# Sixteen gate projections spread anew over the attention units of a two-layer decoder trunk

## The chip, the cores and the metric

One core of one Trainium2 chip. The metric is the device time of one launch in microseconds (us), the median of the runs. Engines: PE (matrix products; PEld is its weight load), DVE (vector), ACT (scalar functions), POOL (GpSimd), SP (issues transfers). PE's clock has two levels, 1.2 and 2.4 GHz; the profile gives the granted share.

## The reference

Two layers, 512 tokens, width 1024, everything in float32:

```python
h = rms_norm(x, g_attn)
proj = h @ w_in                       # dq dk dv sq sk sv gates: 6 x 512 + 2 x 1024 columns
o_diff = diff_attention(...)          # 4 heads: softmax(q1 k1) - lam * softmax(q2 k2), rotary on q and k
o_sb = stick_breaking_attention(...)  # 8 heads: running product of sigmoids along the keys
g_diff, g_sb = split(sigmoid(gates + b_gate))
merged = g_diff * (o_diff @ w_o_diff) + g_sb * (o_sb @ w_o_sb)
x = x + merged @ w_out
gate, up = split(rms_norm(x, g_ffn) @ w_ffn_in)
x = x + (silu(gate) * up) @ w_ffn_out
```

A last RMSNorm ends the trunk.

## The kernel before, in words

All activations lie transposed, with 128 channels on the partitions and the 512 tokens along a row. A product keeps float32 accuracy by splitting both operands into a high and a low part: each 128x512 step is three matmuls (lines 204, 205, 206: high times high, low weight times high, high weight times low). One *group* is 128 output columns over 8 blocks of the input, 24 matmuls of 512 columns into one PSUM bank.

The weights come as one stream of 512 KB pieces in the order of `layer_order`. For each, SP loads `wr`, ACT makes the high part `wh` (line 111), and DVE the low part `wl` (line 113). Of the input projection's pieces every fourth in the stream (`n % 4 == 0`) has its low part made by POOL instead. Two buffers hold `wr`, four each hold `wh` and `wl`, and two pieces are fetched ahead.

In a layer the input projection has 40 groups: three (k, q, v) for each of eight attention *units*, and 16 gate groups. Units s0 to s3 are stick-breaking, with two heads each; d0 to d3 are differential, with one head each. The groups of s0 open the layer. Then come eight *slots*, n = 0 to 7: slot n runs the score maps of unit n, the groups of unit n+1, and, `LAG` = 2 half slots later, the products with v of the unit before. `FILL[n]` says up to how many groups slot n holds; what is left after the three of unit n+1 is filled with gate groups. Gate groups that no slot takes stand in `TAIL`: two go beside the last two half slots, the rest behind all units. The 8 groups `ws`/`wd` of the output projections follow (12 matmuls each), with the sigmoids of the gates, then `w_out` and the FFN.

In `gate_group` (`pg` in the profile) the 24 matmuls fill a bank of tag `mm`, of which there are three, shared with the k, q and v groups. DVE then multiplies the bank by the norm's factor into a tile `gt` (line 321), and that frees the bank. Banks of tag `at` (five) hold scores (`ss`, `sd`), transposes (`ts`, `td`, `vts`, `vtd`), products with v (`avs`, `avd`) and the mean squares (`omd`). In the tile names a final s or d stands for the kind of unit.

The order written in the code is not the order of issue: a planner orders each engine's queue at build time from its own costs, and each engine then runs its queue in order. A matmul whose input is late therefore holds up all matmuls behind it.

Before the change, slots 0 to 3 hold three groups each (no gates), slots 4 to 6 one gate each, slot 7 four, and `TAIL` nine, of which seven stand behind all units. Only the first four gates get a tile of their own (`blk`); later ones reuse tiles of tag `stk`, `klz` and `wk` as units release them.

Of the kernel before, what the change touches and what calls it, by code (L numbers as in the profile page):

```python
# [15 lines left out]
P = 128  # L16
DEPTH = 2
S = 512
# [13 lines left out]
C_NA, C_NF, C_NL, C_BG, C_SL, C_LP = 0, 16, 32, 40, 72, 74  # L32


BUFS = dict(mx=4, sm=4, blk=12, tmp=5, stk=6, v=3, wk=4, wT=3)
BANK_BUFS = dict(mm=3, at=5)
W_BUFS, W_AHEAD = 4, 2
GATES_IN_BLK = 4
FILL = (3, 3, 3, 3, 4, 4, 4, 4)
LAG = 2  # L40


# [5 lines left out]
def trunk(ctx: ExitStack, tc, xT, par, tab, scn, msk, w_in, w_o, w_out, w_fi, w_fo, out):  # L48
    nc = tc.nc
# [6 lines left out]
    def bank(tag, name):  # L56
        return psm.tile([P, 512], F32, name=name, tag=tag, bufs=BANK_BUFS[tag])
# [4 lines left out]
    def unit_groups(u):  # L62
        kind, i = u
        return [("in", c + i) for c in ((4, 0, 8) if kind == "d" else (16, 12, 20))]
# [7 lines left out]
    for n in range(8):  # L72
        g = unit_groups(UNITS[n + 1]) if n < 7 else []
        while len(g) < FILL[n] and gi < len(GATES):
            g.append(GATES[gi])
# [118 lines left out]
    def mm(dst, key, rhs, first=True, last=True):  # L194

        hi, lo = w_get(*key)
        mm_tiles(dst, hi, lo, rhs, first, last)
# [70 lines left out]
    for l in range(DEPTH):  # L268
        h = nrm.h
        with ExitStack() as ac:  # L270
# [10 lines left out]
            def T(tag, name, shape=(P, S), dt=F32):  # L281
                return ap_.tile(list(shape), dt, name=f"{name}_{l}", tag=tag, bufs=BUFS.get(tag, 1))

            def blk(name, dt=F32):
                return T("blk", name, dt=dt)
# [13 lines left out]
                    nc.gpsimd.memset(f32(klz[b][c])[64 - 64 * c:128 - 64 * c], 0.0)  # L299

            gates = {}
            pair = [None]
            TAIL = list(TAIL0)

            def gate_group(key):
                b = bank("mm", f"pg{key[1]}_{l}")
                mm(b, (l,) + key, h)
                j = key[1] - 24
                n = len(gates)
                if n < GATES_IN_BLK:  # L310
                    t = blk(f"gt{j}")
                elif n < GATES_IN_BLK + BUFS["stk"]:
                    t = T("stk", f"gt{j}")
                elif n < GATES_IN_BLK + BUFS["stk"] + 2:
                    t = T(f"klz0{n - GATES_IN_BLK - BUFS['stk']}", f"gt{j}")
                else:
                    q = (n - GATES_IN_BLK - BUFS["stk"]) % 2
                    if q == 0:
                        pair[0] = T("wk", f"gt{j}", (P, 1280))
                    t = pair[0][:, q * S:q * S + S]  # L320
                nc.vector.tensor_tensor(out=t, in0=b, in1=r, op=ALU.mult)
                gates[j] = t

# [220 lines left out]
            def fill(key):  # L544
                n = sum(u.done == 3 for u in units)
                if n < 8 and key in unit_groups(UNITS[n]):
                    units[n].group(key)
                else:
                    gate_group(key)
# [34 lines left out]
            for m in range(8):  # L584
# [11 lines left out]
                nc.vector.tensor_tensor(out=gd, in0=gd, in1=gs, op=ALU.add)  # L596
                if m < 3 or m - 3 < BUFS["wk"] - 2:
                    t = T("wT" if m < 3 else "wk", f"mt{m}", (P, 1280), F32R)
# [122 lines left out]
```

## Time and profile before

| | |
|---|---|
| runs | 1520.3, 1525.24, 1525.61 us; median 1525.24 |
| profiled execution | 1526.8 us, of which the span from first to last instruction is 1525.0 |
| granted PE clock, mean over the span | 0.988 |
| PE busy | 1488.5 us |
| DVE, ACT, POOL busy | 853.7, 614.4, 347.4 us |
| attention stage of layer 0, of layer 1 | about 25 to 314 us, 770 to 1065 us |

How to read it: PE is busy nearly all the time, so what matters is where it stands idle and where it runs at the low clock. Both happen in few places, which a table of busy time by stretch finds. A row of such a table has, after the stretch, its length, and then for each engine the busy time and, in brackets, the number of instructions; then the granted clock, the share of the DMA engines and what they moved.

### The profile page before, as it was taken

What the parts mean: (1) busy time and instruction counts of PE and PEld (TensorE: products, weight loads), DVE (VectorE), ACT (ScalarE), POOL (GpSimd) and SP (SyncE); (2) the same over time, 40 slices, a digit from 0 to 9 for tenths busy, and PEclk for the clock granted to TensorE, in tenths of its full rate; (3) what the DMA queues carried; (4) which work ended last, traced back from release to release, by engine and by line L of the source; (5) the groups of instructions that cost most, each with busy time, mean ns of one, the idle gap of its engine ahead of it and who ended that gap; (6) DMA issues with size and microseconds to landing.
All of it is one profiled execution on the core that took longest, in us unless ns stands there. A gap on an engine that the chain in (4) does not pass through costs nothing.

```text
span 1525.0 us, 17531 instructions
## 1 busy us (share of the span) xinstructions
PE 1488.5 (98%) x6884; PEld 1238.6 (81%) x6884; DVE 853.7 (56%) x1006; ACT 614.4 (40%) x970; POOL 347.4 (23%) x224
## 2 busy tenths in 40 slices
PE   8899999999999999999998999999999999999997
PEld 6788878888888888888877878788888888888886
DVE  5878776475545454433367787655655454544223
ACT  5655544543433232322235655446333232323221
POOL 4345652000111111101124455420021111110011
PEclk9999999999999999999999999999999999999999
DMA  6212222233233233233321223222333233323331
GB/s 208 70 56 82 78 85 88 70 110 97 97 97 97 97 97 97 90 95 95 108 96 45 91 58 97 80 74 83 97 97 97 97 97 97 97 97 91 99 101 56
DMA packets 43619, 139.59 MB, mean 92 GB/s; under 512 B 5648, under 2 KB 8080, under 8 KB 43536
## 3 DMA queue, kind: packets, MB, share of 16 engines
q1 hardware_dynamic: 42240, 137.38, 28.8%
q8 instruction: 54, 0.88, 0.2%
q10 hardware_dynamic: 1296, 1.09, 0.2%
q14 instruction: 29, 0.24, 0.0%
HBM read 132.16 MB, written 2.10 MB: 88 GB/s over the span
## 4 chain that ended last, share of the span: by engine, by line
PE 90%; DVE 5%; issue 1%; ACT 1%; DMA 1%; POOL 0%; SPq 0%; DVEq 0%; POOLq 0%; ACTq 0%
PE fu L206 5%; PE fg L205 5%; PE fg L206 5%; PE fu L205 5%; PE fg L204 5%; PE fu L204 5%; PE fo L204 5%; PE fo L205 5%; PE fo L206 5%; PE pg L204 4%; PE pg L205 4%; PE pg L206 4%; PE pd L204 3%; PE pd L205 3%; PE pd L206 3%; PE wo L204 2%
## 5 line engine op out<-in xcount | busy, mean ns | idle before, releaser
L111 ACT CAST wh<-wr 128x1024 fp32r<-128x1024 f32 (+3 forms) x251 | 258.0, 1029 | 629.7 <-PE fu L206 157.5
L113 DVE TENSOR_TENSOR wl<-wr,wh 128x1024 fp32r<-128x1024 f32 (+2 forms) x229 | 329.8, 1440 | 216.7 <-ACT wh L111 216.1
L626 POOL TENSOR_TENSOR u<-u,g 128x512 f32<-128x512 f32 x44 | 56.8, 1292 | 441.5 <-DVE u L625 394.3
L205 PE MATMUL fo<-ah,wl 128*128 128x512 f32 (+1 forms) x374 | 141.0, 377 | 0.0
L204 PE MATMUL fo<-ah,wh 128*128 128x512 f32 (+1 forms) x374 | 141.0, 377 | 0.0
L206 PE MATMUL fo<-al,wh 128*128 128x512 f32 (+1 forms) x374 | 140.8, 377 | 0.0
L204 PE MATMUL fg<-hhf,wh 128*128 128x512 f32 x352 | 137.8, 391 | 0.0
L206 PE MATMUL fu<-hlf,wh 128*128 128x512 f32 x352 | 137.0, 389 | 0.0
L205 PE MATMUL fg<-hhf,wl 128*128 128x512 f32 x352 | 137.0, 389 | 0.0
L206 PE MATMUL fg<-hlf,wh 128*128 128x512 f32 x352 | 137.0, 389 | 0.0
L204 PE MATMUL fu<-hhf,wh 128*128 128x512 f32 x352 | 137.0, 389 | 0.0
L205 PE MATMUL fu<-hhf,wl 128*128 128x512 f32 x352 | 137.0, 389 | 0.0
L625 DVE TENSOR_TENSOR u<-fu,yf 128x512 f32<-128x512 f32 x44 | 30.4, 691 | 129.2 <-PE fu L206 129.2
L204 PE MATMUL pg<-hha,wh 128*128 128x512 f32 x256 | 100.5, 392 | 0.0
L205 PE MATMUL pg<-hha,wl 128*128 128x512 f32 x256 | 100.3, 392 | 0.0
L206 PE MATMUL pg<-hla,wh 128*128 128x512 f32 x256 | 100.2, 391 | 0.0
L206 PEld LDWEIGHTS fo<-al,wh 128*128 128x128 f32 x374 | 70.4, 188 | 13.0
L205 PEld LDWEIGHTS fo<-ah,wl 128*128 128x128 f32 x374 | 70.4, 188 | 12.9
L204 PEld LDWEIGHTS fo<-ah,wh 128*128 128x128 f32 x374 | 70.4, 188 | 12.9
L113 POOL TENSOR_TENSOR wl<-wr,wh 128x1024 fp32r<-128x1024 f32 (+3 forms) x22 | 51.9, 2360 | 124.9 <-ACT wh L111 120.4
L204 PE MATMUL pd<-hha,wh 128*128 128x512 f32 x192 | 78.2, 407 | 0.5 <-ACT knd3s L341 0.5
L205 PE MATMUL pd<-hha,wl 128*128 128x512 f32 x192 | 77.7, 405 | 0.0
(270 smaller groups left out, 3093.1 us busy)
## 6 DMA issues: line engine op xcount, KB each, us to landing
wr<-in_w_fi_dram SPq DMA_DIRECT2D x88, 512.0 KB, 3.6
wr<-in_w_in_dram SPq DMA_DIRECT2D x78, 512.0 KB, 3.7
wr<-in_w_fo_dram SPq DMA_DIRECT2D x32, 512.0 KB, 3.5
wr<-in_w_o_dram SPq DMA_DIRECT2D x16, 512.0 KB, 3.6
wr<-in_w_out_dram SPq DMA_DIRECT2D x16, 512.0 KB, 3.6
wr<-in_w_fo_dram SPq DMA_DIRECT2D x16, 384.0 KB, 3.1
x<-in_xT_dram SPq DMA_DIRECT2D x8, 256.0 KB, 5.5
cs<-in_tab_dram SPq DMA_DIRECT2D x2, 512.0 KB, 5.4
```

Of the source, the lines that this page charges most:

```text
L111: nc.scalar.copy(out=hi[:, c], in_=raw[:, c])
L113: eng.tensor_tensor(out=lo[:, c], in0=raw[:, c], in1=f32(hi[:, c]), op=ALU.subtract)
L204: nc.tensor.matmul(dst, hi[:, c], rh, start=first and k == 0, stop=False)
L205: nc.tensor.matmul(dst, lo[:, c], rh, start=False, stop=False)
L206: nc.tensor.matmul(dst, hi[:, c], rl, start=False, stop=last and k == n - 1)
L625: nc.vector.tensor_tensor(out=u, in0=bu, in1=r, op=ALU.mult)
L626: nc.gpsimd.tensor_tensor(out=u, in0=u, in1=g, op=ALU.mult)
```

## The change

`FILL` becomes (5, 5, 4, 4, 3, 3, 3, 4): slots 0 and 1 take two gate groups each, slots 2 and 3 one each, slots 4 to 6 none, slot 7 four as before; six are left in `TAIL`, of which four stand behind all units. The pool `blk` grows from 12 tiles to 19 (seven of 2 KB a partition), and the first eleven gates get a tile of their own; the last five use `stk`. The room comes from the area reserved for the descriptors of software-made transfers, which is set to 1024 bytes a partition.

```diff
-BUFS = dict(mx=4, sm=4, blk=12, tmp=5, stk=6, v=3, wk=4, wT=3)
+BUFS = dict(mx=4, sm=4, blk=19, tmp=5, stk=6, v=3, wk=4, wT=3)
...
-GATES_IN_BLK = 4
-FILL = (3, 3, 3, 3, 4, 4, 4, 4)
+GATES_IN_BLK = 11
+FILL = (5, 5, 4, 4, 3, 3, 3, 4)
...
-            pair = [None]
...
                 if n < GATES_IN_BLK:
                     t = blk(f"gt{j}")
-                elif n < GATES_IN_BLK + BUFS["stk"]:
+                else:
                     t = T("stk", f"gt{j}")
-                elif n < GATES_IN_BLK + BUFS["stk"] + 2:
-                    t = T(f"klz0{n - GATES_IN_BLK - BUFS['stk']}", f"gt{j}")
-                else:
-                    q = (n - GATES_IN_BLK - BUFS["stk"]) % 2
-                    if q == 0:
-                        pair[0] = T("wk", f"gt{j}", (P, 1280))
-                    t = pair[0][:, q * S:q * S + S]
                 nc.vector.tensor_tensor(out=t, in0=b, in1=r, op=ALU.mult)
...
-    nc = _bacc.Bacc("TRN2", target_bir_lowering=False, num_devices=1)
+    nc = _bacc.Bacc("TRN2", target_bir_lowering=False, num_devices=1, dynamic_dma_scratch_size=1024)
```

## Rows read from the trace of the kernel before

**Rows 1.** The page, part 1: busy time, share of the span, instructions.
```profile
PE 1488.5 (98%) x6884; PEld 1238.6 (81%) x6884; DVE 853.7 (56%) x1006; ACT 614.4 (40%) x970; POOL 347.4 (23%) x224
```
**Rows 2.** Busy time by stretches of 25 us, those where PE stands idle.
```profile
0.00:25.00 25.00, 18.94 (x70) 13.67 (x71) 16.78 (x23) 14.99 (x26) 13.86 (x19) 0.99 0.63 211
...
50.00:75.00 25.00, 20.49 (x106) 17.10 (x105) 21.30 (x22) 12.49 (x26) 9.84 (x5) 0.94 0.13 43
75.00:100.00 25.00, 22.83 (x109) 19.46 (x109) 19.07 (x21) 15.04 (x31) 10.81 (x6) 0.85 0.21 64
...
775.00:800.00 25.00, 23.44 (x109) 18.71 (x107) 20.70 (x23) 12.53 (x18) 8.63 (x4) 1.00 0.33 106
800.00:825.00 25.00, 19.99 (x95) 16.07 (x96) 21.85 (x16) 15.05 (x30) 10.11 (x6) 0.96 0.13 43
...
875.00:900.00 25.00, 22.29 (x107) 18.63 (x106) 22.14 (x22) 12.93 (x21) 10.87 (x7) 0.86 0.18 57
...
1500.00:1525.00 25.00, 14.62 (x114) 13.71 (x112) 10.05 (x18) 3.63 (x8) 5.42 (x6) 0.89 0.26 85
```
**Rows 3.** Waits of PE from 45 to 95 us: total, times, longest.
```profile
PE ts L425 <- DVE vs L398: 4.0, 1, 4.0
PE avs L460 <- DVE tls L429: 2.2, 1, 2.2
```
**Rows 4.** Busy time by short stretches where PE's granted clock is low.
```profile
72.00:86.00 14.00, 9.96 (x33) 8.34 (x34) 11.21 (x10) 8.55 (x16) 10.23 (x5) 0.63 0.13 37
...
822.00:827.00 5.00, 4.24 (x15) 3.73 (x16) 4.75 (x7) 3.28 (x7) 4.60 (x2) 0.66 0.03 8
884.00:892.00 8.00, 7.17 (x26) 6.36 (x27) 7.97 (x9) 5.55 (x10) 3.12 (x3) 0.57 0.22 68
```
**Rows 5.** DVE in order of time: start, length, line, operation, idle before.
```profile
73.30 0.42 DVE L398 TENSOR_TENSOR vs<-vts,vs 128x256 fp32r<-128x256 f32 x1 [0.44 <-ACT vs L397]
...
73.65 4.17 DVE L446 TENSOR_TENSOR_SCAN es<-es,msc 128x1280 f32<-128x1280 f32 x1
```
**Rows 6.** POOL in order of time, the same stretch.
```profile
72.69 2.45 POOL L448 TENSOR_TENSOR zs<-zs,es 128x1279 f32<-128x1279 f32 x1 [5.85 <-DVE es L446]
```
**Rows 7.** Groups of DVE instructions, 0 to 330 us: busy, mean ns, idle before.
```profile
L113 DVE TENSOR_TENSOR wl<-wr,wh 128x1024 fp32r<-128x1024 f32 (+1 forms) x37 | 52.7, 1426 | 13.7 <-ACT wh L111 13.4
L446 DVE TENSOR_TENSOR_SCAN es<-es,msc 128x1280 f32<-128x1280 f32 x8 | 24.0, 3004 | 7.4 <-ACT es L441 7.4
...
L321 DVE TENSOR_TENSOR gt<-pg,ya 128x512 f32<-128x512 f32 x16 | 10.9, 687 | 18.6 <-PE pg L206 18.6
```
**Rows 8.** The page, part 5: the low parts that POOL makes.
```profile
L113 POOL TENSOR_TENSOR wl<-wr,wh 128x1024 fp32r<-128x1024 f32 (+3 forms) x22 | 51.9, 2360 | 124.9 <-ACT wh L111 120.4
```
**Rows 9.** Busy time by sections of layer 0's attention.
```profile
111.00:147.00 36.00, 36.00 (x192) 30.70 (x191) 29.54 (x29) 22.66 (x41) 20.90 (x11) 1.00 0.25 74
147.00:216.00 69.00, 67.06 (x350) 57.10 (x348) 50.73 (x83) 36.27 (x80) 35.78 (x23) 1.00 0.30 92
...
293.00:314.00 21.00, 21.00 (x94) 17.39 (x93) 12.12 (x15) 17.84 (x28) 0.00 (x0) 1.00 0.29 94
```
**Rows 10.** Gate groups alone: PE, PEld and DVE by section.
```profile
147.00:216.00 69.00, 11.97 (x48) 8.85 (x48) 0.69 (x1) 1.00 0.30 92
...
293.00:314.00 21.00, 21.00 (x93) 17.20 (x92) 2.07 (x3) 1.00 0.29 94
```
**Rows 11.** PE in order of time, slot 6: a gate's end, scores, a wait.
```profile
194.96 0.39 PE L206 MATMUL pg<-hla,wh 128*128 128x512 f32 x1
...
209.81 0.22 PE L410 MATMUL sd<-kad,qad 128*128 128x128 f32 x1
...
214.51 0.50 PE L410 MATMUL sd<-kbd,qbd 128*128 128x512 f32 x1 [1.82 <-ACT pd L488]
```
**Rows 12.** POOL in order of time, slot 6.
```profile
198.70 2.17 POOL L381 TENSOR_TENSOR qbd<-qnd,qbd 64x512 fp32r<-64x512 f32 x1
```
**Rows 13.** DVE in order of time, slot 6.
```profile
218.23 0.68 DVE L321 TENSOR_TENSOR gt<-pg,ya 128x512 f32<-128x512 f32 x1
```

## Prediction

> **What bounds the kernel.** PE sets the time: it is busy for 1488.5 us of a span of 1525.0, DVE for 853.7 [rows 1]. So a change that leaves PE's work as it is can only touch the 36.5 us in which PE stands idle, and the time it loses at the low clock. The table by stretches of 25 us, the next view, shows where that is. The start holds 6.1 us of idle time and the end 10.4; the change touches neither. Of the rest, layer 0 has 4.5 us between 50 and 75 us and 2.2 between 75 and 100, layer 1 has 1.6, 5.0 and 2.7 in its three stretches [rows 2], and slot 6 has one wait of 1.8 us for the exponentials of d2's scores [rows 11], which comes back in layer 1. The reader should note what stands beside the idle time: DVE is busy for 21.3 of 25 us between 50 and 75 and for 22.1 between 875 and 900 [rows 2]. The third view, the waits of PE, names DVE as what ended them: 4.0 us in which the transposes of s0 wait for the copy of a v block, 2.2 in which a product waits for the low part of a transpose [rows 3]. DVE's own order tells why: the copy stands in its queue behind running products along the keys, and ran only at 73.3 us [rows 5]. The fourth view is the granted clock. It falls after such waits: 0.63 from 72 to 86 us, 0.66 and 0.57 in the two stretches of layer 1 [rows 4]; that is the lower of two levels for twice the missing share.
>
> **The change, part by part.**
>
> *Work.* Nothing is added or removed: 16 gate groups a layer before and after, with the same load, `wh`, `wl` and `gt` for each. One group costs PE 24 x 21.0/93 = 5.4 us [rows 10].
>
> *Early gates, slots 0 to 3.* Slots 0 and 1 get two groups each, 10.8 us of PE work, slots 2 and 3 get 5.4. For each group DVE has `gt`, 0.69 us, and where POOL does not do it `wl`, 1.43 on average [rows 7]: 2.1 us against 5.4 of PE. Counting places in the stream, the gates of slots 0 and 1 stand at 6, 7, 11 and 12, those of slots 2 and 3 at 16 and 20; so three of the six low parts are DVE's, and its bill is 6 x 0.69 + 3 x 1.43 = 8.4 us against 32.4 of PE work in the same slots. The wait of 4.0 us in layer 0 was a lag of DVE behind PE of just that length. In the code's order the two gates of slot 0 stand ahead of the transposes that waited; if the planner keeps that order, PE comes to them 10.8 us later and DVE with 2 x 2.1 = 4.2 us more work, a net 6.6 us of slack, against 4.5 + 2.2 = 6.7 us of idle time [rows 2]. So I take these waits to go, and those of layer 1 in the same slots too: its wait between 875 and 900 us lies in slot 3, behind five of the six gates.
> Idle time that can go: 4.5 + 2.2 + 1.6 + 5.0 + 2.7 = 16.0 us [rows 2]. Clock that can come back [rows 4]: from 72 to 86 us the low level holds for 2 x 0.37 x 14 = 10.4 us; taking the 4.0 us of idle time there, less the 2.2 of the second wait, which I count at the full level, PE worked 8.6 us at half speed and lost 4.3. In layer 1, 822 to 827 gives 2 x 0.34 x 5 = 3.4 us, lost 1.7; 884 to 892 gives 2 x 0.43 x 8 = 6.9 us, less 0.8 idle, lost 3.0. Together 9.0, so 25.0 us at most. Between all and nothing I keep back a fifth, 5.0, because the planner, which put these matmuls ahead of their inputs once, can do so again elsewhere.
>
> *A price that may be higher.* The three low parts that fall to POOL are not simply free for DVE. A running product on DVE took 4.17 us beside POOL's product, against a mean of 3.00 [rows 5 to 7], and a POOL low part takes 2.36 [rows 8]. The Trainium skill ("SBUF — State Buffer", summary of rules for kernel authors) says that a DVE operation with two SBUF inputs and a GpSimd operation that reads SBUF block each other fully, the later one waiting. By that page each POOL low part would cost DVE up to its own 2.36 us, an estimate of 7.1 us more a layer, and the early DVE bill would be 15.5 instead of 8.4. The rows agree with its direction (4.17 against 3.00), and either bill stays under 32.4 us of PE work; by the page the early gates would only be worth less in slot 1, where rival two begins.
>
> *The gates taken out of slots 4 to 6.* Before the wait in slot 6 these slots held two gates, 48 matmuls [rows 10]. Without them the section from 147 to 216 us has 67.1 - 12.0 = 55.1 us of PE work; DVE's 50.7 [rows 9] fall by 2 x 2.1 and rise by one low part that moves from POOL (stream places 24 and 28 instead of 16, 20 and 24), to 47.9. That is 87%. The section before, 111 to 147 us, ran at 29.5/36 = 82% with no gate and no idle time [rows 9]; the one from 50 to 75 ran at 85% and stood idle for 4.5 of 25 us [rows 2]. So the bounds are nothing and 55.1 x 0.18 = 9.9 us a layer. For nothing speaks that in slot 6 the last part of d2's q was ready at 200.9 us [rows 12] and the scores began at 209.8 [rows 11]: 8.9 us of slack, more than the gate of 5.4 that goes there. I take 2 us a layer, 4.0, nearer to the section before, which is the same kind of slot. The wait of 1.8 us stays.
>
> *The end of the attention.* Behind the last mean square of d3 (at 293 us) stood 93 gate matmuls, 21.0 us [rows 10]; three groups fewer leave 21.0 - 16.2 = 4.8. In these 21 us ACT did 17.8 us of work [rows 9]: sigmoids, high parts, table load. Four `ws` of 12 matmuls, 2.7 us each, can still run ahead, as they need only stick-breaking units and eight banks. That gives 4.8 + 10.8 = 15.6 us of cover against 17.8. Bounds nothing and 2.2 us a layer; I take 1, 2.0 in all.
>
> *Tiles and scratch.* The gates of slot 7 no longer wait for `stk` tiles; no wait on them shows among PE's, so nothing. The transfers all stand under hardware queues on the page; the smaller area for software-made ones costs nothing.
>
> **Sum.** -25.0 + 5.0 + 4.0 + 2.0 = -14.0 us. The profiled execution took 1526.8 us, so 1512.8; the median lies 1.6 below it, so 1511.2, and I say 1511. Less than 0.5% either way, some 7.6 us, can't be told from no change here.
>
> **The rivals.**
>
> *One: the differential slots give it back.* If slots 4 to 6 behave like 50 to 75 us, 9.9 us a layer: -25.0 + 5.0 + 19.8 + 2.0 = +1.8, near 1527. For it speaks the load of 87%; against it the slack of 8.9 us.
>
> *Two: the early waits only move.* PE gets 10.8 us more work, but the gates run at another place than ahead of the waiting transposes. If four fifths of the 25.0 stay: -5.0 + 4.0 + 2.0 = +1, 1526. Against it: the gates stand ahead of them in the code.
>
> *Three, slower: gates hold the banks.* The gate of slot 5 ended at 195.4 us and DVE emptied its bank at 218.2 [rows 11, 13], 22.9 us later, and there are three `mm` banks. With two gates in a slot, two banks can be held, and k, q and v pass through one. It decides when `gt` comes later than the two groups that the other banks allow, 10.8 us: beyond that PE idles, 22.9 - 10.8 = 12.1 us a slot. In one slot of each layer this gives -14.0 + 24.2 = +10, 1535; in both, 1560. Against it: in slot 5 nobody needed that bank for long, and DVE had idle time in which it could have emptied it.
>
> *Four: more than I take.* All 25.0 go and nothing comes back: 1500; with the waits of slot 6 gone too, some 1493.
>
> **Chances.** My case 0.55 (1501 to 1517), rival one 0.18, two 0.08, three 0.14, four 0.05. Faster: my case and rival four, 0.6; same: one and two, 0.26; slower: 0.14. The range leaves out the farther ends of rivals three and four: 1499 to 1531; that of the likeliest case alone is 1501 to 1517.
>
> **What would show it.** Right: no wait of PE over 1 us between 45 and 130 us and at the same place in layer 1, and a granted clock of 1.00 there; gate groups among the s groups; slots 4 to 6 with at most the old wait; DVE under 80% in slots 0 and 1. Wrong: `gt` long after its group in slots 0 and 1 with k, q or v groups waiting for DVE (rival three); new waits between the scores of d0 and d2 with DVE near 90% (one); the wait for the v copy still there (two); idle PE between the last `pg` and the first `wd` (the end of the attention).

## The result, and the profile after

The changed kernel takes 1548.18 us (median; 1546.94 to 1549.44), against 1525.42 for the kernel before in the same comparison: a ratio of 1.0157, 95% interval 1.0134 to 1.018. I had forecast 1511 with a range up to 1531. It is slower by 22.8 us.

The page's first part for the changed kernel, beside [rows 1]:

```profile
PE 1495.8 (97%) x6884; PEld 1243.0 (80%) x6884; DVE 852.5 (55%) x1006; ACT 613.4 (40%) x970; POOL 349.9 (23%) x224
```

The span is 1547.3 us, so PE stands idle for 51.5 us instead of 36.5, and the same 6884 matmuls keep it busy for 7.3 us longer, which is the low clock. 15.0 and 7.3 are the 22.3 us by which the span grew. DVE's work has not grown. Next, busy time by stretches; the first two and those from 800 to 925 us answer to [rows 2] (layer 1 starts later than before and its first slots hold gates, so the waits that stood at 822 and 884 us stand at 842 and 913), the others are new:

```profile
50.00:75.00 25.00, 23.77 (x125) 19.96 (x124) 21.95 (x18) 13.37 (x27) 10.75 (x4) 1.00 0.18 53
75.00:100.00 25.00, 21.84 (x101) 18.08 (x100) 15.34 (x18) 9.68 (x18) 7.70 (x4) 0.93 0.23 75
237.00:277.00 40.00, 31.68 (x142) 25.77 (x143) 27.85 (x48) 19.72 (x50) 18.67 (x14) 0.87 0.21 66
300.00:328.00 28.00, 23.49 (x106) 19.33 (x105) 11.43 (x16) 17.36 (x26) 0.00 (x0) 0.94 0.17 56
...
800.00:825.00 25.00, 25.00 (x124) 21.01 (x123) 21.06 (x24) 15.28 (x29) 11.67 (x6) 1.00 0.26 91
825.00:850.00 25.00, 22.19 (x103) 18.28 (x102) 20.89 (x16) 11.07 (x19) 11.11 (x6) 0.93 0.29 94
875.00:900.00 25.00, 25.00 (x125) 21.18 (x124) 17.55 (x20) 11.57 (x21) 8.56 (x5) 1.00 0.19 64
900.00:925.00 25.00, 24.28 (x125) 20.38 (x124) 19.50 (x16) 13.71 (x25) 13.42 (x6) 1.00 0.27 85
...
1000.00:1040.00 40.00, 31.93 (x145) 26.35 (x144) 28.76 (x53) 20.20 (x50) 19.15 (x14) 0.87 0.17 53
```

The early stretches improved on the whole: between 50 and 75 us PE is idle for 1.2 us instead of 4.5, at the full clock; between 75 and 100 it is idle for 3.2 instead of 2.2, at a granted clock of 0.93 instead of 0.85. The loss lies later, where the kernel before had nearly none: 8.3 us idle between 237 and 277, with a granted clock of 0.87, and 4.5 between 300 and 328; layer 1 repeats it. The longest waits of PE from 45 to 330 us, beside [rows 3]:

```profile
PE vtd L379 <- DVE vnd L326: 4.7, 1, 4.7
PE ws L204 <- ACT ohs L566: 4.5, 1, 4.5
PE avs L452 <- DVE tls L421: 3.9, 2, 3.2
PE sd L402 <- ACT pd L480: 2.1, 2, 1.8
PE pg L204 <- ACT knd3s L333: 1.2, 1, 1.2
```

The wait of 4.0 us for the v copy in [rows 3] has gone. Two long waits are new. For the first, PE in order of time, the changed kernel; the two `pg` rows are the last matmuls of the gate groups 6 and 7 of layer 0, counted from 0, the first two of slot 7:

```profile
242.44 0.39 PE L206 MATMUL pg<-hla,wh 128*128 128x512 f32 x1
...
248.86 0.39 PE L206 MATMUL pg<-hla,wh 128*128 128x512 f32 x1
253.99 1.09 PE L379 MATMUL vtd<-ident,vnd 128*128 128x128 f32 x4 [4.75 <-DVE vnd L326]
```

and DVE, where d3's v is read and these groups are emptied (`od` is the output of a differential unit):

```profile
253.15 0.69 DVE L326 TENSOR_TENSOR vnd<-pd,ya 128x512 f32<-128x512 f32 x1
...
275.63 0.74 DVE L521 SCALAR_TENSOR_TENSOR od<-ofd,gsub,yod 128x512 f32<-128x512 f32 x1
276.29 1.87 DVE L313 TENSOR_TENSOR gt<-pg,ya 128x512 f32<-128x512 f32 x3
...
296.15 0.75 DVE L521 SCALAR_TENSOR_TENSOR od<-ofd,gsub,yod 128x512 f32<-128x512 f32 x1
296.82 1.88 DVE L313 TENSOR_TENSOR gt<-pg,ya 128x512 f32<-128x512 f32 x3
```

Three `gt` run back to back at 276.3 us, 33 us after group 6 was complete, and directly behind the write of d1's output; the next stand behind d2's output in the same way. Gate tiles and unit outputs have the same tag here, `blk` (the tiles of one tag share its buffers): eight outputs and eleven gates for nineteen buffers, so none had to come free first. In the code d1's output, three gates, d2's output and two gates follow each other under this tag, and DVE wrote them in that order. Until 276 us two of the three `mm` banks are taken; the third holds d3's v until DVE reads it at 253 us. PE has eight gate groups left and no bank to put one in. It stands, then runs one more group (the third of the `gt`) partly at the low clock, then stands again with all three banks full.

The second new wait is at the end. ACT in order of time, the changed kernel:

```profile
314.97 0.63 ACT L153 ACTIVATE yod<-yod 128x512 f32<-128x512 f32 x1
315.62 1.28 ACT L584 ACT_TABLE_LOAD   x1
316.92 0.72 ACT L584 ACTIVATE gt<-gt,pt 128x512 f32<-128x512 f32 x1
...
326.45 0.61 ACT L566 CAST ohs<-os 128x512 fp32r<-128x512 f32 x1
```

The first `ws` needs the high part of s0's output (`ohs`), long ready to be made, but fourteen sigmoids stand ahead of it in ACT's queue.

### The profile page after: what moved, and what is told of

Same layout as the page of the kernel before. It is cut to its first block, busy times and chain, and to the rows that moved or that the text cites. A ratio compares the mean times of both kernels' runs of the same rounds, so it can differ in the third digit from the quotient of the medians.

```text
span 1547.3 us, 17510 instructions
## 1 busy us (share of the span) xinstructions
PE 1495.8 (97%) x6884; PEld 1243.0 (80%) x6884; DVE 852.5 (55%) x1006; ACT 613.4 (40%) x970; POOL 349.9 (23%) x224
## 4 chain that ended last, share of the span: by engine, by line
PE 85%; DVE 7%; ACT 4%; issue 2%; DMA 2%; SPq 0%; POOL 0%; DVEq 0%; ACTq 0%; POOLq 0%
PE fg L205 5%; PE fu L205 5%; PE fg L206 5%; PE fu L206 5%; PE fu L204 5%; PE fg L204 5%; PE fo L204 5%; PE fo L205 5%; PE fo L206 5%; PE pg L204 3%; PE pg L205 3%; PE pg L206 3%; PE pd L205 3%; PE pd L204 3%; PE pd L206 3%
## 5 line engine op out<-in xcount | busy, mean ns | idle before, releaser
L204 PEld LDWEIGHTS fg<-hhf,wh 128*128 128x128 f32 x352 | 66.1, 188 | 14.2 <-issue 0.5
L205 PEld LDWEIGHTS fg<-hhf,wl 128*128 128x128 f32 x352 | 66.1, 188 | 14.1 <-issue 0.5
L204 PEld LDWEIGHTS fu<-hhf,wh 128*128 128x128 f32 x352 | 66.1, 188 | 13.8
```

The costliest lines, as they stand in the source:

```text
L204: nc.tensor.matmul(dst, hi[:, c], rh, start=first and k == 0, stop=False)
L205: nc.tensor.matmul(dst, lo[:, c], rh, start=False, stop=False)
```

## The experiments

Medians and ratios to the kernel before in the same comparison:

| | kernel | us | ratio, 95% interval |
|---|---|---|---|
| | the change | 1548.2 | 1.0157 [1.0134, 1.018] |
| 1 | own tag for the gates, new spread | 1528.5 | 1.002 [1.0011, 1.003] |
| 2 | the change's tiles, old spread | 1542.5 | 1.0117 [1.01, 1.0134] |
| 3 | small scratch alone | 1525.8 | 1.0002 [0.9993, 1.0012] |
| 4 | new spread, old tiles | 1535.4 | 1.0072 [1.0057, 1.0087] |
| 5 | 1 with the parts ahead of the sigmoids | 1525.4 | 1.0003 [0.9993, 1.0013] |
| 6 | the change with the parts ahead | 1534.8 | 1.0065 [1.005, 1.008] |
| 7 | own tag, old spread | 1516.5 | 0.9941 [0.9926, 0.9956] |
| 8 | own tag, four early gates | 1518.2 | 0.995 [0.9935, 0.9965] |
| 9 | 8 with the parts ahead of the sigmoids | 1512.0 | 0.9919 [0.9906, 0.9933] |
| 10 | own tag, two early gates, one in slot 6 | 1523.1 | 0.9994 [0.9985, 1.0003] |
| 11 | own tag, one early, one in slots 4 and 5 | 1529.9 | 1.0045 [1.0031, 1.0059] |
| 12 | the kernel before, its four gate tiles apart | 1517.6 | 0.9947 [0.9926, 0.9967] |

**1. Gates under a tag of their own**, against the change:

```diff
-BUFS = dict(mx=4, sm=4, blk=19, ...)
+BUFS = dict(mx=4, sm=4, blk=8, gt=11, ...)
...
-                    t = blk(f"gt{j}")
+                    t = T("gt", f"gt{j}")
```

> The changed kernel with its first eleven gate tiles under a tag of their own (gt, 11 tiles; blk back to 8), same spread of the gates. Theory held banks: in the changed kernel DVE emptied the gate groups 6 and 7 of layer 0 only 33 and 28 us after their last matmul, right behind the output of d1, because both kinds of tile are granted in one order; meanwhile two of three mm banks were taken and PE stood idle (9.5 us from 237 to 276 us, plus low clock). It expects each gt to follow its group within 5 us in slot 7, the idle time there mostly gone, and 1515 to 1530 us. Theory too little cover: the chain from the scores of d2 to the last mean square of d3 takes some 70 us in both kernels (223 to 293 before, 243 to 314 after), and five gate groups fewer are left to fill it; where the gates stand in it does not matter. It expects 1540 to 1550 us, with the idle time only moved to the end of the units.

1528.5 us: 19.7 us of the loss go with a change that moves no work and no memory. DVE, own-tag kernel, where gate 6 is emptied:

```profile
243.58 0.69 DVE L313 TENSOR_TENSOR gt<-pg,ya 128x512 f32<-128x512 f32 x1 [0.91 <-PE pg L206]
```

It follows its group at once, the other three of slot 7 within 6.1 us, and none of the waits between 240 and 277 us is left. That the missing bank was what stopped PE shows in d3's v: DVE reads it later still here, and PE does not wait for it, since it has a gate group to run.

```profile
256.57 0.69 DVE L326 TENSOR_TENSOR vnd<-pd,ya 128x512 f32<-128x512 f32 x1
```

The theory of too little cover is wrong as the main cause. It is not wrong altogether; the waits of PE from 45 to 345 us now begin with the end of the attention:

```profile
PE wd L204 <- ACT ohd L566: 5.3, 1, 5.3
PE avs L452 <- DVE tls L421: 3.9, 2, 3.2
PE ws L205 <- DVE wl L113: 1.5, 1, 1.5
PE pg L204 <- ACT knd3s L333: 1.2, 1, 1.2
```

**2. The tiles alone**, against the change:

```diff
-FILL = (5, 5, 4, 4, 3, 3, 3, 4)
+FILL = (3, 3, 3, 3, 4, 4, 4, 4)
```

> The changed kernel with the old spread FILL = (3, 3, 3, 3, 4, 4, 4, 4): only the tiles and the scratch differ from before. Theory held banks: gates that had stk tiles before (and were emptied ahead of the output of d1) now wait behind it, so this is slower than before, 1530 to 1545 us. Theory too little cover: the gates stand where they stood, so 1520 to 1530 us.

1542.5 us. The order of the gates is that of the kernel before; only the tiles differ, and that costs 17 us, as the theory of held banks had it. Its DVE shows the same picture as the change, three `gt` behind d1's output:

```profile
251.84 0.74 DVE L521 SCALAR_TENSOR_TENSOR od<-ofd,gsub,yod 128x512 f32<-128x512 f32 x1
252.50 1.87 DVE L313 TENSOR_TENSOR gt<-pg,ya 128x512 f32<-128x512 f32 x3
```

**3. The scratch alone**, against the kernel before:

```diff
-    nc = _bacc.Bacc("TRN2", target_bir_lowering=False, num_devices=1)
+    nc = _bacc.Bacc("TRN2", target_bir_lowering=False, num_devices=1, dynamic_dma_scratch_size=1024)
```

> The kernel before with the smaller scratch alone. Both theories: no difference, 1520 to 1528 us. A third, that the smaller area slows transfers, expects the 1548 us of the change or part of the way there.

1525.8 us, no difference. The third theory is out.

**4. The new spread with the old tiles**, against the kernel before (and the small scratch of 3):

```diff
-BUFS = dict(mx=4, sm=4, blk=12, ...)
+BUFS = dict(mx=4, sm=4, blk=14, ...)
-GATES_IN_BLK = 4
-FILL = (3, 3, 3, 3, 4, 4, 4, 4)
+GATES_IN_BLK = 6
+FILL = (5, 5, 4, 4, 3, 3, 3, 4)
```

> The new spread with the old way of placing tiles: the six early gates in blk (14 tiles), then stk, klz and wk as before; scratch reduced to make room for the two. Theory held banks: the gates of slot 7 stand in stk and are emptied ahead of the output of d1 as before, so 1515 to 1530 us. Theory too little cover: 1540 to 1550 us, since the spread is that of the change.

1535.4 us, between the two expectations. Only the gates from slot 7 on leave `blk`, which saves 13 us against the change. But the 4.7 us wait for d3's v is still there:

```profile
PE vtd L387 <- DVE vnd L334: 4.7, 1, 4.7
PE wd L204 <- ACT ohd L574: 2.1, 1, 2.1
```

The gates of slot 7 stand in `stk` here, a tag that they share with the q and k stacks of the units. Gates 6 and 7 are emptied 14.9 and 9.1 us after their groups, and after POOL has written the last part of d3's q stack (from 254.39 to 256.53 us), which stands ahead of them in the code:

```profile
257.82 1.29 DVE L321 TENSOR_TENSOR gt<-pg,ya 128x512 f32<-128x512 f32 x2
```

That fits the same reading, but no run takes this tag apart.

**5. ACT's order at the end**, against 1:

```diff
-                nc.scalar.copy(out=hi, in_=t)
+                state["part"] = nc.scalar.copy(out=hi, in_=t)
...
+            last_part = state["part"]
             merged = []
...
-                with tc.issue_after(state["exp"].ins):
+                with tc.issue_after(last_part.ins):
```

> The kernel with the gates' own tag (1528.5 us), and in it ACT makes the high parts of all eight unit outputs before it loads the sigmoid table, instead of after most of the sixteen sigmoids. In the own-tag kernel PE stands idle for 5.3 us in each layer until the high part of d3's output, which waits in ACT's queue behind a table load and sixteen sigmoids (11 us). Theory ACT's order: that wait goes, with the low clock after it, 1512 to 1520 us. Theory too little cover: the gates are spent too early, PE then waits for the sigmoids that free the banks of ws instead, and the time stays at 1524 to 1531 us.

1525.4 us, the second expectation, though not for the reason it gave: PE does not wait for a bank but for a weight. ACT in order of time; PE's wait of 6.6 us ends with the first of the two casts in the last row:

```profile
321.53 0.62 ACT L566 CAST ohd<-od 128x512 fp32r<-128x512 f32 x1 [3.00 <-DVE od L521]
322.17 1.28 ACT L585 ACT_TABLE_LOAD   x1
...
333.40 1.28 ACT L213 ACT_TABLE_LOAD   x1
334.70 1.99 ACT L111 CAST wh<-wr 128x1024 fp32r<-128x1024 f32 x2
```

From 322.2 to 334.7 us ACT is taken for 12.5 us by two table loads and sixteen sigmoids. What stands behind them waits, whichever it is; with six gates left for the end PE has not enough to do meanwhile, as its last gate group ends at 304.9 us.

**6. The same edit on the change itself.**

> The changed kernel with ACT's high parts ahead of the sigmoids, nothing else. Theory ACT's order: its wait of 4.5 us at the first ws goes in both layers, with some of the low clock after it, so 1534 to 1541 us; the waits between 237 and 276 us stay, since they come from the tiles. Theory too little cover: 1545 to 1550 us.

1534.8 us, as theory ACT's order had it: the wait for `ohs` is gone, 4.5 us in each layer, and 13.4 us with the clock. The wait for `vnd`, 4.7 us, is still there. The edit that only moved a wait in 5 removes it here, though the spread is the same: held back by the tiles, the last gate group ends at 320.9 us instead of 304.9, while ACT's block of sigmoids ends at 334.8 us, where it ends at 334.7 in 5. So PE has 16 us more of its own work beside that block.

**7. Own tag, old spread**: 1 with the diff of 2.

> The gates' own tag with the old spread (3, 3, 3, 3, 4, 4, 4, 4). Theory held banks: no gate waits behind a unit's output, the early waits are those of the kernel before, so 1520 to 1530 us, and the difference to the own-tag kernel with the new spread (1528.5) tells what the spread itself does. If the new spread saves some 19 us in the early slots and gives as much back at the end, this one has the early waits and a quiet end. Rival: the end is bad here too, because gates that are no longer held back run too early; then 1535 to 1545 us.

1516.5 us, faster than the kernel before and below the range of either theory. It differs from 2 by nothing but the tag: 26 us. And it is 12.0 us below 1, which differs by nothing but the spread. So with the tiles out of the way the new spread is a loss.

**8. Own tag, four early gates**, against 1:

```diff
-FILL = (5, 5, 4, 4, 3, 3, 3, 4)
+FILL = (5, 5, 3, 3, 3, 3, 3, 4)
```

> The gates' own tag with FILL = (5, 5, 3, 3, 3, 3, 3, 4): four early gates instead of six, eight at the end. Theory too little cover at the end: two more groups, 10.9 us, behind the units cover the wait of 5.3 us for d3's high part in each layer, and little is lost in the early slots, so 1513 to 1520 us. If the early slots need all six gates: waits come back in slots 2 and 3 and the time is 1522 to 1530 us.

1518.2 us, in the first range: two groups moved from slots 2 and 3 to the end are worth 10.3 us. In layer 0 3.1 us of waiting for `ohs` remain, in layer 1 nothing.

**9. Both: 8 with the edit of 5.**

> Own tag, four early gates (2, 2, 0, 0, 0, 0, 0, then 4 and 8 at the end: 1518.2 us), with ACT's high parts ahead of the sigmoids. Theory: after the last exponential of d3 ACT is taken for some 12 us by two table loads and sixteen sigmoids whichever way round, so the order of the parts only moves the wait (as with six early gates, where 5.3 us for d3's part became 6.6 for a weight); 1514 to 1520 us, the two waits for ohs in layer 0 (3.1 us) gone or moved. Rival, that the order is the cause: these waits go and nothing comes back, 1512 to 1515.

1512.0 us, 6.2 below 8 and what the rival expected: the wait goes and nothing comes back, since with eight gates left PE has work while ACT makes its sigmoids. My theory, that the order never matters, was too strong: it matters once there is enough cover. This is the fastest kernel of the study. Its longest waits of PE from 45 to 330 us:

```profile
PE avs L452 <- DVE tls L421: 3.6, 2, 3.2
PE avd L506 <- DVE tld L421: 2.5, 1, 2.5
PE pg L204 <- ACT knd3s L333: 1.9, 1, 1.9
```

**10. Two early gates**, against 1:

```diff
-FILL = (5, 5, 4, 4, 3, 3, 3, 4)
+FILL = (4, 4, 3, 3, 3, 3, 4, 4)
```

> Own tag, FILL = (4, 4, 3, 3, 3, 3, 4, 4): one early gate in each of slots 0 and 1, one in slot 6, four in slot 7, nine at the end as in the kernel before. Theory: the end is covered as in the own-tag kernel with the old spread (1516.5), and two early gates take part of the early waits (8.7 us of idle time in layer 0 with no early gate, some 5 with six): 1508 to 1515 us. Rival, that moving gates early always costs as much later: 1516 to 1522.

1523.1 us, a miss. The end is quiet, but the early waits are not between those of none and of six gates: several waits of 1 to 2 us for `tls`, `vs` and `zs`, 10.9 us in all from 45 to 330 us, more than the 6.7 of 7.

**11. One early gate**, against 1:

```diff
-FILL = (5, 5, 4, 4, 3, 3, 3, 4)
+FILL = (4, 3, 3, 3, 4, 4, 3, 4)
```

> Own tag, FILL = (4, 3, 3, 3, 4, 4, 3, 4): one gate early in slot 0, one each in slots 4 and 5, four in slot 7, nine at the end. Theory: the 4.0 us wait of the first transposes and its low clock go, the rest is as with the old spread (1516.5): 1510 to 1515 us. Rival: 1516 to 1522.

1529.9 us, a miss as well. With nine gates behind the last slot PE still waits 4.3 us for `ohs` at the first `ws`, so the number left for the end does not decide alone: d3's last exponential comes at 306.0 us and the last gate group ends at 313.9, 7.9 us later, where the kernel before has 20.3 us between the two (293.9 and 314.2). Early waits remain as well. Why the planner's orders of 10 and 11 come out worse than their neighbours' stays open; I did not take them apart.

**12. The kernel before with its tiles apart:**

```diff
-BUFS = dict(mx=4, sm=4, blk=12, ...)
+BUFS = dict(mx=4, sm=4, blk=8, gt=4, ...)
...
-                    t = blk(f"gt{j}")
+                    t = T("gt", f"gt{j}")
```

> The kernel before with its four gate tiles of tag blk under a tag of their own (gt, 4; blk 8): same spread, same memory, same scratch, stk, klz and wk as before. Theory held banks: in the kernel before the second gate group (slot 5) was already held for 22.9 us behind the output of d0, and its bank is missing where PE waits 1.8 us in slot 6; with the tags apart it is emptied within some 5 us, that wait goes in both layers, and the time comes near the own-tag kernel with the old spread (1516.5): 1514 to 1520 us. Rival: the gain of that kernel came from the larger number of gate tiles (eleven instead of four), not from the tag: 1523 to 1528 us.

1517.6 us, a ratio of 0.9947. The gate of slot 5, emptied 22.9 us late in [rows 13], is now emptied 2 us after its group:

```profile
197.91 0.68 DVE L321 TENSOR_TENSOR gt<-pg,ya 128x512 f32<-128x512 f32 x1
```

and the wait of 1.8 us of [rows 11] is gone from PE's waits. With four gate tiles it comes within 1.1 us of 7, which has eleven, so the number of tiles shows no effect.

## Why the prediction was wrong

**The step that failed is "Tiles and scratch".** I priced the seven new tiles at nothing, because no wait of PE named them. The scratch does cost nothing (3). The tiles cost 17 us with the old spread (2) and 19.7 with the new (1). What the runs show in place of that step: a gate tile under the units' tag is not written before the unit output that stands ahead of it in the code under the same tag, also when tiles are free. In the change and in 2 each late row of `gt` stands right behind such an output; with a tag of its own it stands within 6.5 us of its group (1, 12). The tile holds back the DVE operation, that holds a bank, the bank holds back PE. The kernel before shows the same contrast within itself, in rows that the prediction did not use. DVE there, layer 0:

```profile
242.95 0.69 DVE L321 TENSOR_TENSOR gt<-pg,ya 128x512 f32<-128x512 f32 x1 [4.92 <-PE pg L206]
...
254.98 0.75 DVE L529 SCALAR_TENSOR_TENSOR od<-ofd,gsub,yod 128x512 f32<-128x512 f32 x1
255.64 1.28 DVE L321 TENSOR_TENSOR gt<-pg,ya 128x512 f32<-128x512 f32 x2
```

The gate groups 2 and 3, of slots 6 and 7, whose tiles have the tag `blk`, ended at 228.6 and 235.6 us and were emptied behind d1's output, 27.1 and 20.7 us later. Group 4, the first with a `stk` tile, ended at 242.9 and was emptied at once, so one bank always turned over and PE did not stop: it idles for 0.1 us between 216 and 293 us. (The rows do not number the tiles; which `gt` is which follows from the waits and from the order of the code.) In the change all gates of slot 7 have `blk` tiles, and that last bank was lost too. That the tag's order is the reason is inferred from these orders and from the eight kernels in which the gates have their own.

**Rival three was the mechanism, in another place.** I had seen the bank of slot 5's gate held for 22.9 us and priced two such gates in a slot. It happened, but in slot 7 and not in slots 0 and 1, where one gate of layer 0 was emptied 6.1 us after its group's end and all others of both layers within 3.5. The chance of 0.14 was too low for the reason that I gave against it: DVE had idle time in which it could have emptied the bank. An engine that is free and leaves a finished input lying is held by something else; that should have been followed up, not taken as comfort. Nor was the bank free of use: with the tags apart it is emptied early and the wait of 1.8 us in slot 6 is gone (12). The measured time lies between this rival's two prices, 1535 and 1560, by luck, as they were worked out for slots 0 and 1; both lay outside the stated range, which ended at 1531 although the rival had a chance of 0.14.

**The end of the attention: the term was mis-sized.** I took 1 us a layer with 2.2 as the bound, letting four `ws` run ahead as cover because they need only the stick-breaking units. In the change `ws` itself waited, 4.5 us a layer, since its own input stands behind the sigmoids; in 1 it was `wd`, 5.3 us. The bound left out that a queue runs in order: 12.5 us of sigmoids and table loads count as one block. With the low clock after it this cost 13.4 us in the change (6), not 2.0.

**The early gates: right in kind, too large.** The long wait of layer 0 went, and of that in slot 3 of layer 1 0.7 us were left. But a wait of 3.2 us in layer 0 (2.2 before) and one of 2.8 in layer 1 (3.0 before), both for a low part of a transpose, stayed with a stretch of low clock each (0.93 in the rows above). By the stretches the idle time fell from 16.0 to some 8.6 us (1.2, 3.2 and 0.7 in layer 0, 2.8 and 0.7 in layer 1), the lost clock from 9.0 to about 2 x 0.07 x 25 = 3.5 us of low level a layer, half of it lost, so 3.5: 25.0 became 12.1, where I kept back 5.0. The net 6.6 us of slack was computed for one wait and spent on three.

**Slots 4 to 6 gave nothing back.** I took 2 us a layer. Slot 6 has one wait of 1.2 us, less than the 1.8 before; rival one did not occur.

**Sum.** Early -12.9 instead of -20.0, slots 4 to 6 two times -0.6 of idle time instead of +4.0, the end +13.4 instead of +2.0, the tiles +19.7 instead of nothing: +19 by these, against 22.8 measured; the terms come from different kernels and overlap, so they do not add exactly. Each edit also makes the planner order the queues anew, and 10 and 11 came out 6.6 and 13.4 us above 7 for reasons that stay open in part; a difference of that size between two kernels is not pinned to one term by the times alone.

## What to carry to other kernels

In these kernels a pool tag acts as an order as well as a number of buffers: tiles that are filled at different paces should not share one, however many there are. Parting them gained 7.5 us in the kernel before (12), while the whole respread, with the tiles apart, lost 12.0 (1 against 7). When an operation with a ready input runs late on an idle engine, ask what its output waits for. Work that can fill gaps is worth most where the last long chain ends, so count what must still be hidden there, queue by queue, before spending the filler earlier.

## What the runs showed of the hardware that I had not expected

Waits of under 2 us can be followed by the low clock. In the kernel before, the one wait of 1.8 us in slot 6 [rows 11] stands just ahead of a stretch with a granted clock of 0.57, from 215 to 219 us; in the change the waits of 1.8 and 0.4 us from 270 to 273 stand ahead of one from 273 to 281 (0.57). Not every such wait is: after the wait of 1.2 us at 237 us in the change the clock stays at 1.00, and so it does in the kernel before after waits of 1.6 and 1.0 us in layer 1, at 800 and 807 us. What decides is not shown. The other low stretch in the change, 0.57 from 253 to 261 us, follows the long wait of 4.7 us; together they make the 0.87 between 237 and 277. Over the whole change the clock adds about half of what the waits themselves cost: 7.3 us of longer busy time on 15.0 of idle time.
